# RWKV recurrence of a two-layer trunk: per-pair chunk chain replaced by an affine map per chunk, three head pairs together

## The chip, the cores and the metric

One core of a Trainium2 chip runs the whole program. The metric is device time in microseconds. TensorE (PE) multiplies matrices and loads its stationary operand in separate instructions (PEld); VectorE (DVE) and ScalarE (ACT) do elementwise work; SyncE (SP) issues most DMAs. SBUF and PSUM have 128 partitions; an f32 matmul that is not marked fp32r appears as two MATMUL instructions in the profile, a transpose or an fp32r matmul as one.

## The reference

Two residual layers over 512 tokens of width 1024. The even layer projects the normed input once and splits the columns among MoBA attention (6 heads), RWKV-7 time mixing (6 heads of 64) and memory attention (4 heads); the odd layer has differential attention, HGRN2 and memory attention. The part that is changed is the RWKV recurrence:

```python
def step(st, inp):          # st (head, v, k); all float32
    r_t, w_t, k_t, v_t, a_t, b_t = inp
    sa = jnp.einsum('bhvk,bhk->bhv', st, a_t)
    st = st * w_t[:, :, None, :] + sa[..., None] * b_t[:, :, None, :] + v_t[..., None] * k_t[:, :, None, :]
    return st, jnp.einsum('bhvk,bhk->bhv', st, r_t)
```

with a = -kk, b = kk * a of the layer, a decay w per channel, and after it a group norm per head, a bonus term and a SiLU gate.

## The kernel before

The program is written with a tile framework that orders the instructions of each engine at build time by priority and inserts the waits. The levels, from the first: the RWKV functions run at the top, evictions of projections beside them (`band("e")`), weight loads and their splits next (`band("w")`), norms of attention inputs then (`band("n")`), and projection matmuls (`band("d")`) last, in the order of the string `RWO`. So a projection matmul goes where TensorE has no RWKV instruction to issue.

A projection (`projT`, `projN`, L235) is three fp32r products, hi*hi, hi*lo and lo*hi, each over eight blocks of 128 rows: 24 matmuls of 512 columns for 128 transposed outputs, 96 of 256 columns for a natural chunk. Each chunk of weights is loaded by DMA, split into hi (ACT, L226) and lo (DVE, L227). `RWO` names the chunks: `l0` the low-rank codes and r of pair 0, `k0` k and v of pair 0, `r1` r and k of pair 1, `v1`, `r2`, `v2` likewise; `qm`, `q1` to `q3`, `g0`, `g1` feed attention and gates. The results of r, k, v are evicted by `shift` (L964 on ACT, L968 on DVE). After them, gates `gm` and `ga` are projected in the attention stage, into tiles of a pool that is opened when the RWKV pool is closed.

RWKV handles its six heads as three pairs (two heads of 64 channels on 128 partitions), 512 tokens as 8 chunks of 64. For each pair in turn: `rwkv_prep` builds decays, normed keys, chunk products (L792, L808), masks and transposes; `rwkv_inverse` inverts the 64x64 triangular matrix of each chunk by five doubling levels, two bursts of matmuls each (L856, L863) with VectorE steps between; `rwkv_chain` walks the eight chunks, three 128x128 products a chunk (L888, L894, L900) with evictions between; `rwkv_out` forms the outputs (L914, L916), norms and gates them. The tiles that the next pair needs at once have two buffers, most others one. In the functions below `T`, `V`, `A`, `G` are TensorE, VectorE, ScalarE and GpSimd; `pj("t")` alternates two PSUM tiles, `s2` gives a PSUM tile of two banks.

Of the kernel before, what the change touches and what calls it, by code (L numbers as in the profile page):

```python
# [36 lines left out]
RWO = 'l0 k0 qm r1 v1 q1 r2 g0 v2 q2 q3 g1'  # L37
# [109 lines left out]
def tile_trunk(ctx, tc, x_in, memT_in, w_mem, e_w_in, e_w_out, o_w_in, o_w_out, ln_g, w2_in, a2_in,  # L147
# [588 lines left out]
    def rwkv_prep(rp, q, rkv, lor, rm64, w2a):  # L736
        r, kv = rkv
        k, v = kv[:, :, 0, :], kv[:, :, 1, :]
        t8 = lambda t: t.rearrange("p (c t) -> p c t", t=64)
        bkT = tl(rp, [P, 8, 2, 64], "bkT")  # L740
        a, e2 = bkT[:, :, 0, :], bkT[:, :, 1, :]
        L = tl(rp, [P, S], "lw")
        for m in range(2):
            z = pj("t0")
            T.matmul(z, w2a[:, m, q * P:(q + 1) * P], lor[:, m, :], start=True, stop=True)
            A.activation(a if m else L, t8(z) if m else z, AF.Tanh, scale=0.5, bias=hw0[:, 3 * m + q:3 * m + q + 1])
        A.activation(L, L, AF.Identity, scale=-0.5 * CDEC, bias=ncd)
# [26 lines left out]
        V.tensor_tensor(t8(nr[:, 1]), r, e1[:, :, 1:65], op=OP.mult)
        plc = tl(rp, [P, 8], "plc", bufs=2)
        V.tensor_copy(plc, e1[:, :, 64])
        V.scalar_tensor_tensor(a, a, 1.0, kk, op0=OP.add, op1=OP.mult)
        V.scalar_tensor_tensor(a, a, 0.5, e2, op0=OP.mult, op1=OP.mult)
        V.tensor_tensor(e2, k, e2, op=OP.mult)
        t1 = tl(rp, [P, 8, 64], "t1")  # L780
        V.scalar_tensor_tensor(t1, r, R("rk", q), k, op0=OP.mult, op1=OP.mult)
        bs = pj("t0")
        T.matmul(bs, C("bo"), t1.rearrange("p c t -> p (c t)"), start=True, stop=True)
        bon = tl(rp, [P, S], "bon", bufs=2)
        V.tensor_tensor(t8(bon), t8(bs), v, op=OP.mult)
        hs = [slice(0, 64), slice(64, 128)]
        s = s2()
        for p in range(2):
            for c in range(8):
                o = s[hs[c % 2], p, (c // 2) * 64:(c // 2) * 64 + 64]  # L790
                b_, n_ = bkT[hs[p], c, 0, :], nr[hs[p], 0, c * 64:(c + 1) * 64]
                T.matmul(o, n_ if p else b_, b_ if p else n_, start=True, stop=True)  # L792
        lu = C("lu").rearrange("p (l t) -> p l t", t=64)
        nb = tl(rp, [P, NT, 64], "nb", bufs=2)
        nb2 = tl(rp, [P, NT, 64], "t1")
        sv = s[:, :, 0:256].rearrange("p a (i t) -> p a i t", t=64)
# [3 lines left out]
        nk = tl(rp, [P, 2, 8, 64], "nk")  # L800
        ar = tl(rp, [P, 2, 8, 64], "ar", bufs=2)
        for z in range(2):
            s = s2()
            sv = s.rearrange("p a (c x t) -> p a c x t", x=2, t=64)
            zs = slice(4 * z, 4 * z + 4)
            for c in range(4):
                for p in range(2):
                    T.matmul(sv[:, p, c], bkT[hs[p], 4 * z + c].rearrange("p a t -> p (a t)"),  # L808
                             nr[hs[p], :, (4 * z + c) * 64:(4 * z + c + 1) * 64], start=True, stop=True)
            V.tensor_tensor(nk[hs[1], :, zs], sv[hs[1], :, :, 0, :],  # L810
                            lu[hs[1], 2, None, None, :].to_broadcast([64, 2, 4, 64]), op=OP.mult)
            V.tensor_tensor(ar[:, :, zs], sv[:, :, :, 1, :], C("mr")[:, None, None, :].to_broadcast([P, 2, 4, 64]),
                            op=OP.mult)
        V.tensor_tensor(bkT, bkT, plc[:, :, None, None].to_broadcast([P, 8, 2, 64]), op=OP.mult)
        uv = tl(rp, [P, 2, 8, 64], "uv", bufs=2)
        s = s2()
        sv = s.rearrange("p z (c t) -> p (z c) t", t=P)
        for c in range(8):
            T.transpose(sv[:, c], kv[:, c].rearrange("p a t -> p (a t)"), ident)
        for p in range(2):  # L820
            A.activation(uv[hs[1], p], sv[hs[1], :, hs[p]], AF.Copy)
        bk = tl(rp, [P, 8, P], "bk", bufs=2)
        s = s2()
        sv = s.rearrange("p z (c t) -> p (z c) t", t=P)
        for c in range(8):
            T.transpose(sv[:, c], bkT[:, c].rearrange("p a t -> p (a t)"), ident)
        A.activation(bk.rearrange("p c t -> p (c t)"), s.rearrange("p z t -> p (z t)"), AF.Copy, scale=C("sg"))
        t = pj("t0")
        for p in range(2):
            for c in range(8):  # L830
                m = 4 * p + c // 2
                T.matmul(t[hs[c % 2], m * 64:m * 64 + 64], nk[hs[1], p, c, :], uv[hs[1], p, c, :],
                         start=True, stop=True)
        nv = tl(rp, [P, 8, 64], "nv", bufs=2)
        A.activation(nv.rearrange("p m t -> p (m t)"), t, AF.Copy)
        return dict(bon=bon, nr=nr, pl=plc, nb=nb, nv=nv, ar=ar, uv=uv, bk=bk)

    def rwkv_inverse(rp, st):
        E = st["nb"]
        hs = [slice(0, 64), slice(64, 128)]  # L840
        f = lambda t: t.rearrange("p i t -> p (i t)")
        f3 = lambda t: t.rearrange("p (i t) -> p i t", t=64)
        cm = lambda n, l: C(n).rearrange("p (l t) -> p l t", t=64)[:, l, None, :].to_broadcast([P, NT, 64])
        xx = tl(rp, [P, NT, 64], "xx", bufs=2)
        F = tl(rp, [P, NT, 64], "F", bufs=2)
        V.tensor_tensor(xx, E, cm("lev", 0), op=OP.mult)
        V.tensor_tensor(F, cm("i64", 0), xx, op=OP.subtract)
        for l in range(1, 6):
            R1 = tl(rp, [P, NT, 64], "R1")
            R2 = tl(rp, [P, NT, 64], "R2")  # L850
            V.transpose(f(R1), f(F))
            V.tensor_tensor(R1, R1, cm("tri2", l - 1), op=OP.mult)
            x = pj("t1")
            for i in range(NT):
                for h in hs:
                    T.matmul(x[h, i * 64:i * 64 + 64], E[h, i, :], R1[h, i, :], start=True, stop=True)  # L856
            V.tensor_tensor(R2, F, cm("tri2", l - 1), op=OP.mult)
            xx = tl(rp, [P, NT, 64], "xx", bufs=2)
            V.tensor_tensor(xx, f3(x[:, :256]), cm("lev", l), op=OP.mult)
            x = pj("t1")  # L860
            for i in range(NT):
# [12 lines left out]
        V.tensor_tensor(g64[:, :, 0], F, cm("lu", 0), op=OP.mult)
        A.activation(g64[:, :, 1], f3(x[:, :256]), AF.Copy)
        st["g64"] = g64

    def rwkv_chain(rp, st, Z, Wz):
        hs = [slice(0, 64), slice(64, 128)]
        uv, bk, nr, pl, g64 = st["uv"], st["bk"], st["nr"], st["pl"], st["g64"]  # L880
        nv = st["nv"].rearrange("p (a i) t -> p a i t", a=2)
        cs_ = st["c"] = s2("c")
        for c in range(8):
            i, h = c // 2, c % 2
            W = Wz[h]
            if c:
                w = cs_[:, 0, 0:P]
# [525 lines left out]
```

## Time and profile before

| | us |
|---|---|
| median of 3 runs | 695.09 (694.81 to 695.23) |
| the profiled execution | 695.85 |
| its span, first to last instruction | 694.1 |
| TensorE matmul busy / weight loads | 669.2 (96%) / 557.3 (80%) |
| VectorE / ScalarE busy | 505.5 (73%) / 336.5 (48%) |

A row of a group names line, engine, operation, tiles (out<-in) and shapes (for a matmul stationary rows*columns, output partitions x moving columns), how often, then busy us and mean ns of one, then the idle time before it and what ended it. Matmuls overlap in TensorE's pipeline, so the mean of one is its latency; what it costs in a stream is the distance of starts, which the timeline gives.

### The profile page before, as it was taken

The page shows a single profiled execution, that of the slowest core. Times are in us where ns is not written, and L with a number is a line of the kernel's source. Part 1 is how long each engine was busy: PE and PEld are TensorE (multiplying, and loading weights), DVE is VectorE, ACT ScalarE, POOL GpSimd, SP SyncE. Part 2 cuts the span into 40 slices and gives each one's busy share as a digit, 9 for nine tenths or more (in the row PEclk, how much of TensorE's full clock was granted, in tenths as well). Part 3 has the DMA queues.
Part 4 walks back from the last instruction along what each step waited for, and adds up shares of the span by engine and source line. Part 5 has one row for each costly group of instructions (what it writes and reads, how often), then busy time and mean ns, then how long its engine had stood idle before and what let it go on. Part 6 is the DMA issues. An engine that isn't in the chain of part 4 may idle for free.

```text
span 694.1 us, 14695 instructions
## 1 busy us (share of the span) xinstructions
PE 669.2 (96%) x5748; PEld 557.3 (80%) x5748; DVE 505.5 (73%) x1487; ACT 336.5 (48%) x1009; POOL 7.2 (1%) x24
## 2 busy tenths in 40 slices
PE   8899999999999998999999999899999999999998
PEld 5777877787679876566799988679999977567997
DVE  3996876988795759857765985994737558889853
ACT  5567245262334347534532866544445336568520
POOL 1000000000000000000000000000000000000000
PEclk9999999999999999999999999999999999999999
DMA  8372122111013242010342344003324231000223
GB/s 300 112 192 61 32 61 79 45 35 43 20 36 89 62 126 88 1 38 1 111 161 87 122 128 109 16 3 122 120 64 119 65 92 31 31 1 1 92 61 122
DMA packets 62903, 53.48 MB, mean 77 GB/s; under 512 B 3377, under 2 KB 61041, under 8 KB 62834
## 3 DMA queue, kind: packets, MB, share of 16 engines
q1 hardware_dynamic: 62834, 52.55, 24.8%
q8 instruction: 45, 0.74, 0.5%
q14 instruction: 24, 0.20, 0.1%
HBM read 50.44 MB, written 2.10 MB: 76 GB/s over the span
## 4 chain that ended last, share of the span: by engine, by line
PE 71%; DVE 16%; ACT 7%; issue 2%; DMA 2%; SPq 0%; ACTq 0%; DVEq 0%
PE pj L235 49%; PE s L466 2%; PE c L900 1%; PE t L863 1%; PE t L520 1%; PE t L572 1%; PE t L856 1%; DVE lo L227 1%; ACT pr L547 1%; PE t L1278 1%; PE t L512 1%; PE c L894 1%; PE t L449 1%; DVE act_lo L425 1%; DMA memT<-in_memT_dram 1%
## 5 line engine op out<-in xcount | busy, mean ns | idle before, releaser
L226 ACT ACTIVATE hi<-raw 128x512 fp32r<-128x512 f32 (+2 forms) x164 | 90.7, 597 | 85.4 <-PE pj L235 65.3
L227 DVE TENSOR_TENSOR lo<-raw,hi 128x512 fp32r<-128x512 f32 (+2 forms) x164 | 102.0, 648 | 28.0 <-PE pj L235 24.5
L235 PE MATMUL pj<-hi,act_hi 128*128 128x256 f32 x672 | 105.9, 286 | 0.7 <-ACT act_hi L274 0.5
L235 PE MATMUL pj<-hi,act_lo 128*128 128x256 f32 x672 | 105.3, 285 | 0.0
L235 PE MATMUL pj<-lo,act_hi 128*128 128x256 f32 x672 | 104.7, 285 | 0.0
L235 PEld LDWEIGHTS pj<-hi,act_hi 128*128 128x128 f32 x672 | 90.2, 188 | 3.3 <-ACT act_hi L274 1.2
L235 PEld LDWEIGHTS pj<-hi,act_lo 128*128 128x128 f32 x672 | 90.1, 188 | 1.0 <-issue 0.4
L235 PEld LDWEIGHTS pj<-lo,act_hi 128*128 128x128 f32 x672 | 90.0, 188 | 0.7 <-issue 0.2
L235 PE MATMUL pj<-act_hi,lo 128*128 128x512 f32 (+1 forms) x248 | 73.9, 415 | 0.0
L235 PE MATMUL pj<-act_lo,hi 128*128 128x512 f32 (+1 forms) x248 | 73.8, 415 | 0.0
L235 PE MATMUL pj<-act_hi,hi 128*128 128x512 f32 (+1 forms) x248 | 69.1, 406 | 0.0
L235 PEld LDWEIGHTS pj<-act_lo,hi 128*128 128x128 f32 (+1 forms) x248 | 44.4, 189 | 11.5 <-issue 1.6
L235 PEld LDWEIGHTS pj<-act_hi,hi 128*128 128x128 f32 (+1 forms) x248 | 44.4, 187 | 9.9 <-issue 0.5
L235 PEld LDWEIGHTS pj<-act_hi,lo 128*128 128x128 f32 (+1 forms) x248 | 44.3, 189 | 9.9 <-issue 1.2
L586 DVE TENSOR_TENSOR x<-pj,x 128x256 f32<-128x256 f32 x64 | 27.0, 422 | 34.7 <-PE pj L235 34.5
L617 ACT ACTIVATE sq<-pj 128x64 f32<-128x64 f32 x144 | 30.1, 226 | 26.7 <-DVE nat L492 15.5
L478 ACT ACTIVATE pr<-pr,mx 128x128 f32<-128x128 f32 (+3 forms) x56 | 30.9, 556 | 4.4 <-DVE mx L476 4.0
L617 ACT ACTIVATION_READ_ACCUMULATOR sq<-pj 128x1 f32 x144 | 29.3, 211 | 0.0
L476 DVE CUSTOM_DVE_ANT_0 pr<-s,mask 128x128 f32<-128x128 f32 (+3 forms) x56 | 25.7, 484 | 4.2 <-PE t L512 1.9
L490 ACT ACTIVATE uv<-c 64x64 f32<-64x64 f32 x48 | 10.5, 219 | 34.9 <-PE c L894 34.3
L490 ACT ACTIVATE PT<-t 128x512 f32<-128x512 f32 (+3 forms) x28 | 13.9, 497 | 26.4 <-PE t L563 9.7
L547 ACT ACTIVATE pr<-s,mmx 128x256 f32<-128x256 f32 x32 | 14.8, 484 | 7.6 <-DVE mmx L544 7.6
(388 smaller groups left out, 1087.8 us busy)
## 6 DMA issues: line engine op xcount, KB each, us to landing
raw<-in_o_w_in_dram SPq DMA_DIRECT2D x20, 512.0 KB, 3.7
raw<-in_e_w_in_dram SPq DMA_DIRECT2D x36, 256.0 KB, 3.3
raw<-in_e_w_in_dram SPq DMA_DIRECT2D x10, 512.0 KB, 5.0
x<-in_x_dram SPq DMA_DIRECT2D x8, 512.0 KB, 7.7
raw<-in_o_w_in_dram SPq DMA_DIRECT2D x16, 256.0 KB, 3.6
raw<-in_o_w_out_dram SPq DMA_DIRECT2D x8, 512.0 KB, 3.4
raw<-in_e_w_out_dram SPq DMA_DIRECT2D x4, 512.0 KB, 3.5
raw<-in_w_mem_dram SPq DMA_DIRECT2D x4, 512.0 KB, 3.5
```

The source lines that it names most:

```text
L226: A.activation(hi[:, z, :n], r, AF.Copy)
L227: V.tensor_tensor(lo[:, z, :n], r, hi[:, z, :n].bitcast(F32), op=OP.subtract)
L235: T.matmul(o, lh(k), rh(k), start=c == 0, stop=c == tot - 1)
L425: V.tensor_tensor(act_lo[:, k0:k0 + 4, i * P:(i + 1) * P], tv, hv.bitcast(F32), op=OP.subtract)
L449: T.transpose(t[:, i * P:(i + 1) * P], nat[:, i, c0:c0 + P], ident)
L466: T.matmul(o, qT[a][h, qs], kT[b][h, ks], start=c == 0, stop=c == 2)
L476: V.tensor_tensor_reduce(pr[:, p, :n], s[:, p, :n], mask[0][:, 384 - i * P:512], 1.0, 1e38, op0=OP.add, op1=OP.min, accum_out=mx[:, p:p + 1])
L478: A.activation(pr[:, p, :n], pr[:, p, :n], AF.Exp, bias=mx[:, p:p + 1], scale=-1.0, accum_out=rs[:, p:p + 1])
L490: A.activation(dst, src, AF.Copy)
L547: A.activation(pv[:, p, ii, :], sv[:, p, ii, :], AF.Exp, bias=mx[:, c:c + 1], scale=-1.0, accum_out=rs[:, c:c + 1])
L586: V.tensor_tensor(x[i][:, cs], o, x[i][:, cs], op=OP.add)
L617: A.activation(sq[:, h0 + h], o[:, 64 * (h0 + h):64 * (h0 + h + 1)], AF.Square, accum_out=ss[:, i * nh + h:i * nh + h + 1])
```

## The change

Each chunk's effect on the state is written as an affine map: state' = AT^T state + Z. `rwkv_prep` builds what the maps need for one pair, into tiles `X` that hold all three pairs; the three preparations run first. Then `rwkv_inverse` inverts the chunks of all pairs in one batch (24 blocks in a burst instead of 8), `rwkv_affine` multiplies the inverses out into AT, Z, corrected r and Y, `rwkv_chain` needs one product and one add for each chunk, for three pairs at once, and `rwkv_out` runs for each pair. `RWO` moves `qm`, `q1` and `g0` behind the chunks of r, k and v. The r and k tiles have two buffers, v one. Three memsets on GpSimd go. Added and context lines of the diff, cut to its core (removed lines stand in the functions above):

```diff
+RWO = 'l0 k0 r1 v1 r2 v2 qm q1 g0 q2 q3 g1'
...
+    def rwkv_tiles(rp):
+        return dict(nr=tl(rp, [P, 4, S], "nr3"), pl=tl(rp, [P, 3, 8], "pl3"), bon=tl(rp, [P, 3, S], "bon3"),
+                    nb=tl(rp, [P, 3, NT, 64], "nb3"), NN=tl(rp, [P, 3, 2, NT, P], "NN3"),
+                    BA=tl(rp, [P, 3, 2, NT, P], "BA3"), Z=tl(rp, [P, 3, 7, 64], "Z3"),
+                    Yv=tl(rp, [P, 3, 2, NT, 64], "Yv3"))
+
+    def rwkv_prep(pp, X, q, rkv, lor, rm64, w2a):
...
+        cz = lambda i, h: slice((2 * i + h) * 64, (2 * i + h) * 64 + 64)
+        s = s2("s")
+        sv = s.rearrange("p a (i t) -> p a i t", t=P)
+        for i, h, p in rows:
+            nc_ = cz(i, h)
+            if p:
+                T.matmul(sv[hs[h], p, i, 0:64], n[hs[p], nc_], b[hs[p], nc_], start=True, stop=True)
+                T.matmul(sv[hs[h], p, i, 64:P], b[hs[p], nc_], rs[hs[p], nc_], start=True, stop=True)
+            else:
+                T.matmul(sv[hs[h], p, i], b[hs[p], nc_], nr[hs[p], 0:q + 2:q + 1, nc_], start=True, stop=True)
...
+        V.tensor_tensor(BA[:, :, :, 64:P], sv[:, :, :, 64:P], lub(0), op=OP.mult)
+        s = s2("c")
+        sv = s.rearrange("p a (i t) -> p a i t", t=P)
+        for i, h, p in rows:
+            T.matmul(sv[hs[h], p, i], e2[hs[p], cz(i, h)], nr[hs[p], 0:q + 2:q + 1, cz(i, h)], start=True, stop=True)
+        nk = tl(pp, [P, 2, NT, 64], "t1", bufs=4)
+        V.tensor_tensor(nk, sv[:, :, :, 0:64], lub(2), op=OP.mult)
+        av = tl(pp, [P, 2, NT, 64], "t1", bufs=4)
+        V.tensor_tensor(av, sv[:, :, :, 64:P], lub(0), op=OP.mult)
...
+        for f, dst in ((n, NN[:, :, :, 64:P]), (b, BA[:, :, :, 0:64]), (e2, None)):
+            t = pj("t")
+            for i in range(NT):
+                T.transpose(t[:, i * P:(i + 1) * P], f[:, i * P:(i + 1) * P], ident)
+            if dst is None:
+                A.activation(kt.rearrange("p i t -> p (i t)"), t, AF.Copy)
+            else:
+                A.activation(dst, i2(t), AF.Copy)
+        ph_ = lambda t, p, i: t[:, (p * NT + i) * 64:(p * NT + i) * 64 + 64]
+        for src, dst in ((nk, NN[:, :, :, 0:64]), (av, X["Yv"][:, q])):
+            t = pj("t")
+            for i, h, p in rows:
+                T.matmul(ph_(t, p, i)[hs[h]], src[hs[h], p, i], vt[hs[h], i, hs[p]], start=True, stop=True)
+            A.activation(dst, p2(t), AF.Copy)
+        s = s2("s")
+        for i, h, p in rows:
+            if 2 * i + h < 7:
+                T.matmul(s[hs[p], h, i * 64:i * 64 + 64], kt[hs[h], i, hs[p]], vt[hs[h], i, hs[p]],
                          start=True, stop=True)
...
+        xx, F, R1, R2 = (T4(n) for n in ("xx", "F", "R1", "R2"))
+        V.tensor_tensor(xx, E4, cm("lev", 0), op=OP.mult)
         V.tensor_tensor(F, cm("i64", 0), xx, op=OP.subtract)
         for l in range(1, 6):
...
+            x = x4()
+            for j in range(2 * J):
                 for h in hs:
+                    T.matmul(at(x, h, j), E[h, j], at(R1, h, j), start=True, stop=True)
...
+            for j in range(2 * J):
                 for h in hs:
+                    T.matmul(at(x, h, j), at(xx, h, j), at(R2, h, j), start=True, stop=True)
+            V.tensor_tensor(F, F, x, op=OP.subtract)
...
+                        X["pl"].rearrange("p q c -> p (q c)")[:, :, None].to_broadcast([P, 24, 64]), op=OP.mult)
+        rows = [(i, h, p) for i in range(NT) for p in range(2) for h in range(2)]
+        for q in range(3):
+            NN, BA = X["NN"][:, q], X["BA"][:, q]
+            s = s2("s")
+            for i, h, p in rows:
+                T.matmul(s[hs[h], p, i * P:(i + 1) * P], g[hs[h], q * NT + i, p], NN[hs[h], p, i],
                          start=True, stop=True)
             for p in range(2):
+                o = s[:, p].rearrange("p (i t) -> p i t", t=P)
+                if p:
+                    V.tensor_scalar(NN[:, p], o, -1.0, None, op0=OP.mult)
+                else:
+                    A.activation(NN[:, p], o, AF.Copy, scale=-1.0)
+        for q in range(3):
+            NN, BA = X["NN"][:, q], X["BA"][:, q]
+            s = s2("c")
+            for i, h, p in rows:
+                T.matmul(s[hs[p], h, i * P:(i + 1) * P], NN[hs[h], p, i, 64:P], BA[hs[h], p, i], start=True, stop=True)
+            sv = s.rearrange("p h (i t) -> p h i t", t=P)
+            s = s2("s")
+            for i, h, p in rows:
+                if 2 * i + h < 7:
+                    T.matmul(s[hs[p], h, i * 64:i * 64 + 64], BA[hs[h], p, i, 0:64], NN[hs[h], p, i, 0:64],
+                             start=True, stop=True)
+            d = AT[:, q].rearrange("p (i h) t -> p h i t", h=2)
+            V.tensor_tensor(d, sv[:, :, :, 0:64], d, op=OP.add)
+            for h in range(2):
+                z = X["Z"][:, q, h:7:2]
+                V.tensor_tensor(z, s[:, h, 0:64 * z.shape[1]].rearrange("p (i t) -> p i t", t=64), z, op=OP.add)
+            d = X["nr"][:, q + 1].rearrange("p (i h t) -> p h i t", h=2, t=64)
+            V.tensor_tensor(d, sv[:, :, :, 64:P], d, op=OP.add)
+            t = pj("t").rearrange("p (a i t) -> p a i t", a=2, t=64)
+            for i, h, p in rows:
+                T.matmul(t[hs[h], p, i], BA[hs[h], p, i, 64:P], NN[hs[h], p, i, 0:64], start=True, stop=True)
+            V.tensor_tensor(X["Yv"][:, q], t, X["Yv"][:, q], op=OP.add)
+        return AT
+
+    def rwkv_chain(X, AT):
+        Z = X["Z"]
+        s = s2("s")
+        for c in range(1, 7):
+            o = s[:, c % 2, 0:192].rearrange("p (q t) -> p q t", t=64)
+            for q in range(3):
+                for h in hs:
+                    T.matmul(o[h, q], AT[h, q, c], Z[h, q, c - 1], start=True, stop=True)
+            V.tensor_tensor(Z[:, :, c], o, Z[:, :, c], op=OP.add)
...
+        s = s2("sc"[q % 2])
+        y = s[:, :, 0:256].rearrange("p a (i t) -> p a i t", t=64)
...
+        for c in range(1, 8):
             for p in range(2):
+                T.matmul(y[hs[c % 2], p, c // 2], X["nr"][hs[p], q + 1, c * 64:(c + 1) * 64], X["Z"][hs[p], q, c - 1],
+                         start=True, stop=True)
...
+                                got[n, q] = d = tl(pp, [P, S], n, bufs=1 if n == "v" else 2)
...
             for q in range(3):
+                rwkv_prep(pp, X, q, [got[n, q] for n in "rkv"], lor, rm64, w2a)
+            pps.close()
+            with ExitStack() as ips:
+                ip = pool(ips, "ip")
+                AT = rwkv_affine(ip, X, rwkv_inverse(ip, X))
+                rwkv_chain(X, AT)
+                for q in range(3):
+                    rwkv_out(ip, X, q, sg[3 + q])
```

## Rows read from the trace of the kernel before

**Rows 1.** The page: the engines' busy time, share of the span and instructions.

```profile
PE 669.2 (96%) x5748; PEld 557.3 (80%) x5748; DVE 505.5 (73%) x1487; ACT 336.5 (48%) x1009; POOL 7.2 (1%) x24
```

**Rows 2.** Stretches of the span. Columns: stretch and its length, busy time of each engine (instructions), granted clock, share of DMA, GB/s.

```profile
55.00:262.00 207.00, 202.55 (x1918) 163.78 (x1919) 158.33 (x459) 87.22 (x266) 1.65 (x5) 1.00 0.21 60
262.00:345.00 83.00, 79.52 (x471) 54.35 (x470) 61.75 (x170) 44.10 (x127) 0.00 (x0) 1.00 0.13 38
```

**Rows 3.** Groups of TensorE matmuls from 55 to 262 us, L235 being the projections: one row of three for 512 columns (x96, x96, x94) and one of three for 256 columns (x128 each).

```profile
L235 PE MATMUL pj<-act_hi,lo 128*128 128x512 f32 x96 | 29.5, 417 | 0.0
...
L235 PE MATMUL pj<-lo,act_hi 128*128 128x256 f32 x128 | 21.9, 293 | 0.0
```

**Rows 4.** Timeline of TensorE where projections run alone. Columns: start, duration to the modelled end of the last, engine, line, operation, tiles, stationary and moving shapes, count.

```profile
298.78 2.03 PE L235 MATMUL pj<-act_hi,lo 128*128 128x512 f32 x8
300.65 2.03 PE L235 MATMUL pj<-act_hi,hi 128*128 128x512 f32 x8
...
364.75 0.76 PE L235 MATMUL pj<-hi,act_lo 128*128 128x256 f32 x5
365.35 0.76 PE L235 MATMUL pj<-lo,act_hi 128*128 128x256 f32 x5
```

**Rows 5.** The same timeline at a burst of the inverse (L856 and L863 are its two products), and where one stands beside the 16 instructions of L832: the rows left out are single instructions of both.

```profile
152.48 0.63 PE L235 MATMUL pj<-act_lo,hi 128*128 128x512 f32 x2
153.04 0.68 PE L863 MATMUL t<-R,xx 64*64 64x64 f32 x16
153.65 0.74 PE L235 MATMUL pj<-act_lo,hi 128*128 128x512 f32 x2
...
86.56 0.51 PE L832 MATMUL t<-uv,nk 64*64 64x64 f32 x10
...
87.64 0.62 PE L235 MATMUL pj<-hi,act_lo 128*128 128x256 f32 x3
```

**Rows 6.** The same timeline in the first steps of the first pair's chain.

```profile
106.21 1.17 PE L235 MATMUL pj<-act_hi,lo 128*128 128x512 f32 x4
107.29 0.49 PE L900 MATMUL c<-uv,bk 128*128 128x128 f32 x2
107.53 0.94 PE L235 MATMUL pj<-act_hi,lo 128*128 128x512 f32 x3
108.42 0.49 PE L888 MATMUL c<-Z,nr 128*128 128x128 f32 x2
108.66 0.48 PE L235 MATMUL pj<-act_hi,lo 128*128 128x512 f32 x1
108.97 0.62 PE L235 MATMUL pj<-act_hi,hi 128*128 128x512 f32 x2
109.44 0.41 PE L894 MATMUL c<-W,g 128*128 128x128 f32 x2
109.60 0.72 PE L235 MATMUL pj<-act_hi,hi 128*128 128x512 f32 x2
```

**Rows 7.** The same timeline at the first pair's output, with a burst of the second pair's preparation (L808) behind it, and before these L792 of the first pair (the first of its rows, 32 instructions in all, and the projection after them).

```profile
72.92 0.51 PE L792 MATMUL s<-nr,bkT 64*64 64x64 f32 x10
...
73.83 0.73 PE L235 MATMUL pj<-hi,act_lo 128*128 128x256 f32 x4
...
133.32 1.20 PE L914 MATMUL c<-uv,ar 128*64 128x64 f32 x32
134.45 0.68 PE L916 MATMUL c<-Z,nr 64*64 64x64 f32 x28
135.06 1.16 PE L808 MATMUL s<-nr,bkT 64*128 64x128 f32 x16
136.15 0.68 PE L856 MATMUL t<-R,nb 64*64 64x64 f32 x16
```

**Rows 8.** Groups of VectorE and ScalarE from 55 to 262 us. After the bar: busy us and mean ns of one, idle time before them.

```profile
L904 DVE SCALAR_TENSOR_TENSOR Z<-Z,plc,c 64x64 f32<-64x64 f32 x36 | 10.0, 279 | 7.4 <-PE c L900 6.8
L859 DVE TENSOR_TENSOR xx<-t,cmr 128x256 f32<-128x256 f32 x15 | 6.3, 419 | 4.3 <-PE t L856 4.3
L812 DVE TENSOR_TENSOR ar<-s,cmr 128x512 f32<-128x512 f32 x6 | 4.1, 691 | 0.1
L814 DVE TENSOR_TENSOR bkT<-bkT,plc 128x1024 f32<-128x1024 f32 x3 | 3.6, 1214 | 0.0
...
L490 ACT ACTIVATE uv<-c 64x64 f32<-64x64 f32 x48 | 10.5, 219 | 34.9 <-PE c L894 34.3
```

**Rows 9.** Where the pairs stand: first and last start of the first matmul of a preparation (L745), of its last copy (L835) and of the shifts that evict r, k and v (L964), with min/median/max ns; then single rows of the timeline: first and last instruction of the first pair's inverse, one of the last two of its output, and the last pair's last.

```profile
L745 PE MATMUL t<-lor,w2a x6: 394/485/502, 55.2 to 147.2; 96*128 96x512 f32 x6
L835 ACT ACTIVATE nv<-t x3: 590/592/596, 87.7 to 209.4; 128x512 f32<-128x512 f32 x3
L964 ACT ACTIVATE th<-pj,prm x10: 668/690/692, 48.2 to 202.5; 128x512 f32<-128x512 f32 x9, 64x512 f32<-64x512 f32 x1
...
79.05 0.45 DVE L851 STREAM_TRANSPOSE R<-F 128x256 f32<-128x256 f32 x1
105.38 0.39 ACT L875 ACTIVATE g<-t 128x256 f32<-128x256 f32 x1 [4.58 <-PE t L873]
145.35 0.65 DVE L938 TENSOR_TENSOR Yq<-Yq,bon 128x512 f32<-128x512 f32 x1
260.95 0.68 DVE L939 SCALAR_TENSOR_TENSOR sg<-Yq,sg 128x512 f32<-128x512 f32 x1
```

More of the change, by code (lines that the diff above doesn't have):

```diff
@@ L774, in rwkv_prep @@
[L774 to L778, printed above, removed]
+        V.tensor_tensor(t8(n), t8(kk), e1[:, :, 0:64], op=OP.mult)
+        V.tensor_tensor(t8(rs), t8(r), e1[:, :, 1:65], op=OP.mult)
+        V.tensor_copy(X["pl"][:, q], e1[:, :, 64])
+        V.scalar_tensor_tensor(b, b, 1.0, kk, op0=OP.add, op1=OP.mult)
@@ L779, in rwkv_prep @@
+        V.scalar_tensor_tensor(b, b, 0.5, e2, op0=OP.mult, op1=OP.mult)
         V.tensor_tensor(e2, k, e2, op=OP.mult)
-        t1 = tl(rp, [P, 8, 64], "t1")
+        t1 = tl(pp, [P, S], "t1", bufs=4)
         V.scalar_tensor_tensor(t1, r, R("rk", q), k, op0=OP.mult, op1=OP.mult)
[L782 to L796, printed above, removed]
+        bs = pj("t")
@@ new lines, in rwkv_prep @@
+        T.matmul(bs, C("bo"), t1, start=True, stop=True)
+        V.tensor_tensor(X["bon"][:, q], bs, v, op=OP.mult)
+        vt = tl(pp, [P, NT, P], "lw")
+        t = pj("t")
+        for i in range(NT):
+            T.transpose(t[:, i * P:(i + 1) * P], v[:, i * P:(i + 1) * P], ident)
+        A.activation(vt.rearrange("p i t -> p (i t)"), t, AF.Copy)
+        cz = lambda i, h: slice((2 * i + h) * 64, (2 * i + h) * 64 + 64)
+        s = s2("s")
+        sv = s.rearrange("p a (i t) -> p a i t", t=P)
@@ L799, in rwkv_prep @@
         V.tensor_tensor(nb, nb, nb2, op=OP.add)
[L800 to L832, printed above, removed]
-                         start=True, stop=True)
-        nv = tl(rp, [P, 8, 64], "nv", bufs=2)
@@ L857, in rwkv_inverse @@
             V.tensor_tensor(R2, F, cm("tri2", l - 1), op=OP.mult)
[L858 to L861, printed above, removed]
+            V.tensor_tensor(xx, x, cm("lev", l), op=OP.mult)
+            x = x4()
+            for j in range(2 * J):
                 for h in hs:
-                    T.matmul(x[h, i * 64:i * 64 + 64], xx[h, i, :], R2[h, i, :], start=True, stop=True)
@@ new lines, in rwkv_inverse @@
+            V.tensor_tensor(F, F, x, op=OP.subtract)
+        g = tl(ip, [P, 2, J, 2, 64], "g64")
+        V.tensor_tensor(xx, F, cm("lu", 1), op=OP.mult)
+        x = x4()
+        for j in range(2 * J):
+            for h in hs:
+                T.matmul(at(x, h, j), at(xx, h, j), ident[h, h], start=True, stop=True)
+        V.tensor_tensor(g[:, :, :, 0], F, cm("lu", 0), op=OP.mult)
+        for z in range(2):
+            A.activation(g[:, z, :, 1], x[:, z], AF.Copy)
+        return g.rearrange("p b j a t -> p (b j) a t")
```

185 lines of the change are left out of this document (68 added, 117 removed).

## Prediction

> **What bounds the kernel now.** I read the page first. TensorE is busy 96% of the span [rows 1]. "Busy" is not proof, because the ends of matmuls are modelled, so I looked at start-to-start times in the stretch that the change rewrites: from 55 us, when the first head pair's preparation starts, to 262 us, when the last pair's result is written [rows 2, 9]. In those 207 us the granted clock is 1.00, TensorE's upper level of 2.4 GHz, VectorE is busy 158 us, ScalarE 87 us and DMA 21% [rows 2]; none is full. TensorE issues 286 projection matmuls of 512 columns and 384 of 256 there (the two rows shown and the four like them) [rows 3]. In a stretch with no other work such a matmul follows the last one after 0.234 us (8 in 1.87) and 0.120 us (5 in 0.60) [rows 4]. That makes 286 x 0.234 + 384 x 0.120 = 113 us of projection and leaves 94 us. The RWKV bursts fill nearly all of that, as the bursts costed below show: projections run right up to each burst and right after it. So before 262 us TensorE's queue is the bound, the recurrence's long dependency chain is covered by projections, and an RWKV edit is worth the TensorE time that it takes out or puts in, as long as its own chain ends in time. After 262 us comes the attention stage; TensorE is busy 79.5 of 83 us there [rows 2].
>
> **The price of a burst.** All times are from the last projection start before a burst to the first after it, less 0.234 per projection. An f32 matmul is two instructions. An inverse burst is 16 instructions of 64x64 on two quadrants of the array (rows 0-63 to columns 0-63, and the other halves): 153.65 - 152.48 - 2 x 0.234 = 0.70 us, of which 0.61 from its first start to the next projection [rows 5]. Thirty-two such instructions in a row take 1.08 us, so 16 more cost 0.47: 0.029 each, on top of a fixed 0.15 plus 0.09 at the switch. Where four quadrants take turns, 28 instructions need only 0.61 us (L916), so (0.61 - 0.15) / 28 = 0.017 each [rows 7]. A chain burst, two 128x128 instructions, costs 0.38, 0.43 and 0.24 us in the three shown [rows 6]; over the 52 of the trace that stand alone between projections I count a mean of 0.30, which I take.
>
> **The change, part by part (TensorE, three pairs).**
> *Inverse.* 33 bursts of 16 become 11 of 48, the same instructions: 33 x 0.70 = 23.1 before, 11 x (48 x 0.029 + 0.24) = 17.9 after: **-5.2**.
> *Chain.* 22 bursts a pair, 66 x 0.30 = 19.8, go. Six steps remain for all three pairs, each 12 instructions of 64x64 on two quadrants: 6 x (12 x 0.029 + 0.25) = 3.6: **-16.2**.
> *Output.* L914 and L916 take 135.06 - 133.32 = 1.74 us a pair, L916 alone 0.61 [rows 7]; only its like remains: **-3.4**.
> *Preparation.* Gone a pair: L792 0.91, L808 twice 1.09 [rows 7], L832 1.08 (32 instructions of the inverse's kind), with 0.1 for each switch 4.6. New: the products for `s` (per quadrant pair 32 in a row, 1.08), `e2` on four quadrants (32, 0.69), `nk` and `av` times `vt` (1.08 each), `kt` times `vt` (28 on four, 0.63), with switches 5.1. Transposes stay 16 a pair. **+1.4**.
> *Affine map, new.* A pair: `g` times `NN` 1.08, `NN` times `BA` 0.69, `BA` times `NN` 0.63 and 1.08, switches 0.4: 3.9. **+11.6**.
> Sum: **-11.8 us**.
>
> Of these the unknown is the 64x64 matmul with 128 moving columns (`e2`, half of `s`, `g` times `NN`, `NN` times `BA`), which the trace lacks. Nearest from above is L808, 64 rows by 128 stationary and 128 moving columns: 16 instructions in 1.09 us [rows 7], 0.06 each. At that price a pair costs 1.3 more in `e2`, 1.3 in `NN` times `BA`, 0.9 in `g` times `NN`, 0.3 in `s`: +11.3 in all, and the gain is 0.5. Nearest from below is 0.017 and 0.029. I take the low prices: the projection of 256 moving columns issues every 0.120 us, hardly more than the 0.107 that its columns take at 2.4 GHz, so the load of its 128 stationary columns is hidden, and a load should be here too [rows 4].
> The Trainium skill says otherwise ("TensorE: Matmul & The Clock Gate", Part 3, What overlaps and what doesn't): a weight load overlaps a running matmul only when the row group differs. By that rule load and moving columns add up in each row group and the sum would be near the -0.5; by the rows it is -11.8. The trace speaks against the rule: L235 uses all rows in both, and is not slowed to the sum of the two.
>
> *VectorE and ScalarE.* Inverse: 87 instructions of 0.42 become 29 of 768 elements, by interpolation between 0.42, 0.69 and 1.21 for 256, 512 and 1024 elements some 0.96 [rows 8]: 36.5 to 27.8. Masks: four of 0.69 a pair become three. The chain's 17.4 (10.0 of it L904) becomes 16.7 of affine, chain and output adds. VectorE -11 us; ScalarE loses 48 copies of 0.22 and three wide copies [rows 8] and gains eight a pair, about -7. I cost both at nothing, as TensorE's 113 us of projections cover them; without that cover they would only help.
> *Order.* `qm`, `q1` and `g0` move behind the r, k, v chunks of pairs 1 and 2. The same projections, weight loads on SP's queue (two DMAs each), splits on ScalarE and VectorE, and `qm`'s evictions, squares and norms are issued, only later; `qm` is first needed after 262 us. Nothing, covered by DMA at 21%.
> *New waits.* `v` has one buffer, so v of the next pair is shifted only after the last pair's transposes of v; behind that wait on ScalarE stand weight splits and the preparation's own activations. Two projection accumulators let TensorE go on by one output. ScalarE idles 120 of 207 us, so I take nothing; the price is in the second rival.
>
> **Does the chain end in time?** The first preparation runs from 55.2 to 88.3, 33 us; the third is under way at 147 and ends at 210, as it waits for r, k, v projections, whose last shift is at 202.5 [rows 9], and these now come first. VectorE's part is about 15 us a pair: some fifteen instructions of 512 elements at 0.69, L814's 1.21, the scan and a dozen small ones [rows 8]. Three in turn, 28 to 33 each, end at 139 to 154. One pair's inverse took 79.1 to 105.8 [rows 9], 26.7 us, of which its own instructions on the path are about 16 and waits 10.7; in lockstep 5 x (4 x 0.96 + 2 x 1.54) + 3 + 10.7 = 48. Affine: VectorE 3.5 a pair (its adds at the widths of rows 8) and four bursts in turn, 18. Chain: six steps at 1.2 (22 bursts fill 106 to 133 before [rows 6, 7]), 7. Output: 12.7 for one pair (133.3 to 146.0 [rows 7, 9]), of which VectorE 6.6 with the new add; three 12.7 + 2 x 6.6 = 26. Sum 99 us, so it ends at 238 to 253, beside 250 for TensorE's sum (262 - 12) and 262 before. Filler lasts: about 60 of the 113 us remain at 145.
>
> **Rivals.**
> *Wide products at L808's price:* gain 0.5, 694.6. For it only that row; against it rows 4.
> By the rule of the Trainium skill named above ("TensorE: Matmul & The Clock Gate", Part 3) this is what happens.
> *Lockstep comes too late (slower).* No inverse step starts before the third preparation ends, so single buffers (`bkT`, `lw`, `e1`, `v`) in series set the end. It decides from a preparation of 36 us on (55 + 3 x 36 + 99 = 262). At 40 the end is 274, TensorE runs dry and the time is 695.1 + 12 = 707. For it: 33 us is close, and later pairs took longer; against it: those waited for projections.
> *The recurrence ends later than TensorE's sum but before 262,* at about 256: gain 5, 690.
> *More:* the recurrence ends near 238 and attention starts among projections, so part of the waits there (0.5 to 0.9 us each, the 3.5 idle us of rows 2 and as much hidden) goes too: 18 to 24 less, about 674.
>
> **How the numbers follow.** The profiled execution took 695.85 us, span 694.1; the median is 695.09. 695.85 - 11.8 = 684.05, less 0.76 gives 683.3, so **683 us**. Chances: forecast (677 to 688) 0.53, wide products 0.12, too late 0.13, ends at 256 0.10, more 0.12. The range leaves out most of "too late" and the end of "more": 671 to 695. A measurement tells a change from none at about 0.2%, 1.4 us. Faster: 0.53 + 0.10 + 0.12 and a third of the wide products, 0.79; same 0.08; slower 0.13.
>
> **What would show it.** Right: inverse bursts of 48 in about 1.55 us; six chain bursts of 0.35 to 0.6; `e2` and `NN` times `BA` at 32 in 0.7; the last output near 250, with projections around every burst. Wrong: 32 wide instructions in 1.9 us; TensorE idle before the inverse with the third preparation past 163 us; the RWKV stretch shorter, but attention longer by as much because its projections were used up.

## The result, and the profile after

The changed kernel takes 678.77 us (median of 4, 678.45 to 679.95), the kernel before beside it 695.16: ratio 0.9761, 95% interval 0.9739 to 0.9784. The profiled execution took 678.45 us, 17.4 less than that of before; TensorE is as full as it was [rows 1].

The page's busy line (engine, busy us, share, instructions), then two stretches of the span (end times, length, busy us of PE, PEld, DVE, ACT and POOL, TensorE's clock, DMA share, GB/s): the recurrence to its end, and the attention stage. They answer to [rows 1, 2].

```profile
PE 651.4 (96%) x6192; PEld 551.8 (82%) x6192; DVE 491.7 (73%) x1394; ACT 328.2 (49%) x969; POOL 6.8 (1%) x21
...
55.00:249.00 194.00, 189.40 (x2379) 162.01 (x2379) 144.97 (x365) 77.90 (x223) 2.39 (x5) 1.00 0.23 62
249.00:332.00 83.00, 79.72 (x487) 55.29 (x486) 62.88 (x174) 45.84 (x132) 0.00 (x0) 1.00 0.18 60
```

Busy shares hide where the 17 us went, so here is the timeline at the new bursts: the first matmul of the first preparation, the last burst of the third; an inverse burst; the affine map's three kinds; one output; the last instruction of the recurrence. They answer to [rows 5 to 7, 9].

```profile
54.28 0.70 PE L760 MATMUL t<-lor,w2a 96*128 96x512 f32 x2 [0.80 <-DVE w2a L997]
...
136.58 0.63 PE L847 MATMUL s<-lw,t 64*64 64x64 f32 x26
137.15 1.22 PE L235 MATMUL pj<-lo,act_hi 128*128 128x256 f32 x8
...
143.21 1.61 PE L876 MATMUL c<-R,nb 64*64 64x64 f32 x48
144.75 1.10 PE L235 MATMUL pj<-lo,act_hi 128*128 128x256 f32 x7
...
190.89 1.75 PE L905 MATMUL s<-NN,g 64*64 64x128 f32 x28
192.56 0.98 PE L235 MATMUL pj<-lo,act_hi 128*128 128x256 f32 x6
...
197.76 1.64 PE L905 MATMUL s<-NN,g 64*64 64x128 f32 x26 [0.77 <-DVE NN L910]
...
204.61 1.10 PE L917 MATMUL c<-BA,NN 64*64 64x128 f32 x32 [0.29 <-DVE nr L930]
205.51 0.61 PE L922 MATMUL s<-NN,BA 64*64 64x64 f32 x26
...
217.47 0.68 PE L953 MATMUL s<-Z,nr 64*64 64x64 f32 x28
218.08 0.39 PE L235 MATMUL pj<-hi,act_lo 128*128 128x256 f32 x1
...
248.59 0.69 DVE L975 SCALAR_TENSOR_TENSOR sg<-Yq,sg 128x512 f32<-128x512 f32 x1
```

Read start to start: 48 inverse instructions last 144.75 - 143.21 = 1.54 us; 28 wide ones of `g` times `NN` 192.56 - 190.89 = 1.67; 32 wide ones on four quadrants 0.90. Projections stand around the bursts, and the recurrence ends at 249.3 instead of 261.6.

Where the time went, from the first preparation to the first transposes of the odd layer's HGRN2 (55.2 to 420.8 us before, 54.3 to 403.2 after). For each TensorE instruction I took the time to the next one's start, apart from waits over 0.15 us. A burst is whatever TensorE does between two projections, RWKV's or not. A projection counts 0.113 or 0.222 us, the least steady spacing of its two sizes; what exceeds that is booked to the switch into a burst (last projection before it), to the restart (first projection after it), or to the rest. Worked out from the traces, us:

| | before | after | order alone (e2) | old order (e1) | inverse by pair (e3) | pair by pair (e8) |
|---|---|---|---|---|---|---|
| RWKV instructions | 71.5 | 63.9 | 78.2 | 66.1 | 67.3 | 68.5 |
| switches into bursts | 14.2 | 7.5 | 12.1 | 6.8 | 9.7 | 12.0 |
| restarts after bursts | 12.5 | 7.0 | 10.5 | 6.3 | 8.8 | 10.8 |
| bursts | 142 | 79 | 126 | 70 | 96 | 112 |
| projections | 204.2 | 204.2 | 204.2 | 204.2 | 204.2 | 204.2 |
| their other excess | 9.6 | 11.2 | 10.0 | 11.9 | 10.6 | 11.4 |
| other TensorE work | 46.1 | 47.1 | 46.4 | 48.3 | 46.9 | 46.6 |
| waits | 7.5 | 8.1 | 7.7 | 24.1 | 10.7 | 9.2 |
| total | 365.6 | 348.9 | 369.1 | 367.7 | 358.1 | 362.7 |

Before to after: -7.6 in RWKV instructions, -6.7 in switches, -5.5 in restarts, +3.1 elsewhere. Sixty-three bursts fewer are worth 12.2 us apart from the instructions in them.

### The profile page after: what moved, and what is told of

Read it like the earlier page. It is cut to its first block, busy times and chain, and to the rows that moved or that the text cites. A ratio compares the mean times of both kernels' runs of the same rounds, so it can differ in the third digit from the quotient of the medians.

```text
span 676.2 us, 15423 instructions
## 1 busy us (share of the span) xinstructions
PE 651.4 (96%) x6192; PEld 551.8 (82%) x6192; DVE 491.7 (73%) x1394; ACT 328.2 (49%) x969; POOL 6.8 (1%) x21
## 4 chain that ended last, share of the span: by engine, by line
PE 71%; DVE 17%; ACT 6%; DMA 3%; issue 2%; SPq 0%; ACTq 0%; DVEq 0%
PE pj L235 50%; PE s L466 3%; DMA raw<-in_e_w_in_dram 2%; DVE lo L227 1%; PE t L1306 1%; PE t L520 1%; PE t L572 1%; ACT pr L547 1%; PE s L882 1%; PE c L876 1%; PE t L512 1%; PE t L449 1%; PE t L842 1%; DVE pr L554 1%; ACT hi L226 1%
## 5 line engine op out<-in xcount | busy, mean ns | idle before, releaser
L235 PE MATMUL pj<-hi,act_hi 128*128 128x256 f32 x672 | 104.2, 285 | 0.7 <-ACT act_hi L274 0.5
L235 PE MATMUL pj<-hi,act_lo 128*128 128x256 f32 x672 | 102.8, 284 | 0.0
L235 PE MATMUL pj<-lo,act_hi 128*128 128x256 f32 x672 | 102.2, 284 | 0.0
L235 PEld LDWEIGHTS pj<-hi,act_hi 128*128 128x128 f32 x672 | 89.7, 188 | 3.5 <-ACT act_hi L274 1.2
L235 PEld LDWEIGHTS pj<-hi,act_lo 128*128 128x128 f32 x672 | 89.2, 188 | 1.0 <-issue 0.5
L235 PEld LDWEIGHTS pj<-lo,act_hi 128*128 128x128 f32 x672 | 88.9, 188 | 0.8 <-issue 0.3
L235 PE MATMUL pj<-act_lo,hi 128*128 128x512 f32 (+1 forms) x248 | 71.0, 409 | 0.0
L235 PE MATMUL pj<-act_hi,lo 128*128 128x512 f32 (+1 forms) x248 | 69.5, 409 | 0.0
L235 PE MATMUL pj<-act_hi,hi 128*128 128x512 f32 (+1 forms) x248 | 67.7, 403 | 0.0
L235 PEld LDWEIGHTS pj<-act_hi,lo 128*128 128x128 f32 (+1 forms) x248 | 45.7, 190 | 11.2 <-issue 1.2
L235 PEld LDWEIGHTS pj<-act_hi,hi 128*128 128x128 f32 (+1 forms) x248 | 45.0, 187 | 10.6 <-issue 0.5
L235 PEld LDWEIGHTS pj<-act_lo,hi 128*128 128x128 f32 (+1 forms) x248 | 44.6, 187 | 10.7 <-issue 0.5
L429 ACT ACTIVATE th<-pj 128x512 f32<-128x512 f32 x16 | 9.5, 596 | 30.6 <-PE pj L235 30.6
L547 ACT ACTIVATE pr<-s,mmx 128x256 f32<-128x256 f32 x32 | 14.7, 482 | 7.4 <-DVE mmx L544 7.4
```

What stands on the lines that cost most here:

```text
L235: T.matmul(o, lh(k), rh(k), start=c == 0, stop=c == tot - 1)
L429: A.activation(th, o, AF.Tanh, scale=0.5)
L547: A.activation(pv[:, p, ii, :], sv[:, p, ii, :], AF.Exp, bias=mx[:, c:c + 1], scale=-1.0, accum_out=rs[:, c:c + 1])
```

## The experiments

All against runs of the kernel before on the same chip. The diffs are cut to their core.

| kernel | median us | ratio to before, 95% interval |
|---|---|---|
| after | 678.77 | 0.9739 to 0.9784 |
| e1_old_order | 699.83 | 1.0021 to 1.0079 |
| e2_order_alone | 699.54 | 1.0014 to 1.0069 |
| e8_pair_old_order | 692.14 | 0.9919 to 0.9960 |
| e9_pair_new_order | 696.73 | 0.9974 to 1.0035 |
| e3_pair_inverse | 689.67 | 0.9847 to 0.9946 |
| e4_more_projection | 692.04 | 0.9915 to 0.9979 |
| e5_more_bursts | 700.85 | 1.0044 to 1.0094 |
| e6_no_out_norm | 676.85 | 0.9700 to 0.9786 |
| e7_affine_two_psum | 676.76 | 0.9700 to 0.9762 |
| e10_split_wide | 678.47 | 0.9697 to 0.9774 |
| e11_sum_fp32r | 678.33 | 0.9707 to 0.9762 |
| e12_sum_one_burst | 679.13 | 0.9730 to 0.9778 |

**Does TensorE's work decide, or the recurrence's own chain?** Two kernels add work beside that chain, one shortens it by leaving out the group norm of the output.

```diff
 # e4_more_projection, in the outputs of qm, q1, q2, q3
+for _ in range(8):
+    T.matmul(o, lh(k), rh(k), start=True, stop=True)
 # e5_more_bursts, at every sixth step of the same outputs
+T.matmul(scratch, ident[0:64, 0:64], ident[0:64, 0:64], start=False, stop=False)
 # e6_no_out_norm, in rwkv_out
-mu = tl(sp, [P, 8], "ymu")
...
-V.tensor_tensor(Y, Y, r[:, :, None].to_broadcast([P, 8, 64]), op=OP.mult)
```

> The changed kernel with work added: in each of 16 outputs of qm, q1, q2 and q3 the first projection matmul is issued 8 times more (it starts the accumulation anew each time, so the result stays), 128 matmuls of 256 or 512 columns. They stand in the stream of projections beside the recurrence and are on no chain of it. Theory A: all of it shows, 128 x 0.113 to 0.234, 14 us or more (15 if all are of 256 columns). Theory B (the recurrence's chain decides, TensorE has slack): 0 to 3 us.

Measured +13.3 us (ten runs, 690.4 to 695.9). In the trace 128 x 0.113 = 14.5 us of projection came in and 1.6 us of waits went.

> The changed kernel with work added: in the 16 outputs of qm, q1, q2 and q3 a lone f32 product of 64x64 (two instructions) that nobody reads is put after every sixth projection step, 64 bursts in all. It measures what a burst costs that does nearly no work. My prediction's price of a burst, 0.24 fixed plus 2 x 0.029 = 0.30: 64 x 0.30 = 19 us more. With the restart of the projection after it, which the prediction left out, 0.40: 25.6 us more. If a burst costs only its instructions: 64 x 0.06 = 4 us. Theory B (the recurrence's chain decides): 0 to 3 us.

Measured +22.1 us for 64 bursts of two instructions.

A lone burst between projections in that trace (timeline):

```profile
150.39 0.28 PE L239 MATMUL pj<-hi,act_lo 128*128 128x256 f32 x1
150.59 0.33 PE L237 MATMUL pj<-cident 64*64 64x64 f32 x2
150.85 0.97 PE L239 MATMUL pj<-hi,act_lo 128*128 128x256 f32 x6
```

The projection before it takes 0.20 instead of 0.113 to its successor, the two instructions 0.26. Over all, by the same booking as in the table: +14.7 us between starts of other TensorE instructions, which the lone ones are (0.23 a burst), +5.0 in switches, +5.3 in restarts: 25.0 us, 0.39 a burst, of which 2.6 us of waits and 1.2 of other excess are paid back. My price gave 0.30; the restart, which it left out, is the difference.

> The changed kernel without the group norm of the recurrence's output (mean, variance and scaling left out, three times twelve instructions on VectorE and ScalarE; TensorE keeps its instructions). The recurrence's end comes some 10 to 15 us earlier. Theory A (TensorE's work counts): 0 to 2 us faster. Theory B (the recurrence's end counts): 10 to 15 us faster.

Measured -1.9 us, the upper end of theory A; its interval overlaps that of the changed kernel, so the gain is not clear of noise. The first two outputs end at 226.0 instead of 239.2 and attention's first scores start at 228.9 instead of 249.9 us, yet the last instruction comes only 1.7 us earlier in the trace. That the recurrence would end 10 to 15 us earlier failed, it ends at 245.4, since the last output now waits for the gate that it is multiplied with, whose projection is the last of the list:

```profile
243.99 0.69 DVE L430 SCALAR_TENSOR_TENSOR sg<-th,pj 128x512 f32<-128x512 f32 x1 [3.41 <-ACT th L429]
244.71 0.69 DVE L963 SCALAR_TENSOR_TENSOR sg<-Yq,sg 128x512 f32<-128x512 f32 x1
```

**Which part of the change gains: the order, the affine map, or the lockstep?** Each alone:

```diff
 # e1_old_order: after with the order of before; e2_order_alone: before with this order
-RWO = 'l0 k0 r1 v1 r2 v2 qm q1 g0 q2 q3 g1'
+RWO = 'l0 k0 qm r1 v1 q1 r2 g0 v2 q2 q3 g1'
 # e8_pair_old_order, e9_pair_new_order: after, pair by pair (tiles for two pairs, not three)
 for q in range(3):
     rwkv_prep(pp, X, q, [got[n, q] for n in "rkv"], lor, rm64, w2a)
-AT = rwkv_affine(ip, X, rwkv_inverse(ip, X))
-rwkv_chain(X, AT)
-for q in range(3):
+    g = tl(ip, [P, NT, 2, 64], "g64")
+    rwkv_inverse(ip, X, q, g)
+    rwkv_chain(X, q, rwkv_affine(ip, X, q, g))
     rwkv_out(ip, X, q, sg[3 + q])
 # e3_pair_inverse: after, with only the inverse by pair
+for q in range(3):
+    rwkv_inverse(ip, X, q, g)
```

> The changed kernel with the chunks in the order of the kernel before (qm and q1 ahead of the r, k, v chunks they stood ahead of, v2 late); the RWKV code stays new. Theory A (TensorE's work counts, and the recurrence's chain only if it ends after its projections are used up): TensorE's work is the same, so as long as projections last the time is within 1 us of the changed kernel. The third preparation now waits for about 34 us more of projections and ends near 172 instead of 138 us; the 111 us from there to the end of the recurrence (138 to 249 in the changed kernel) then end near 283, projections are used up before, and TensorE idles: 695 to 710, 15 to 30 us above the changed kernel. Theory B (only the chain's end counts): the same direction, the full 34 us, 713. If the order does not matter at all: 678 to 680.

Measured 699.8, 21 us above the changed kernel: theory A. The third preparation ends at 169.4 and the recurrence at 276 (forecast 172 and 283). Windows of the trace (columns as above):

```profile
255.00:262.00 7.00, 0.29 (x3) 0.05 (x1) 6.37 (x19) 1.82 (x3) 0.00 (x0) 0.84 0.40 116
262.00:275.00 13.00, 4.59 (x17) 2.99 (x17) 8.64 (x23) 2.93 (x5) 0.00 (x0) 0.50 0.16 50
275.00:277.00 2.00, 2.00 (x5) 1.36 (x5) 2.00 (x4) 1.04 (x2) 0.00 (x0) 0.53 0.30 121
277.00:290.00 13.00, 11.61 (x91) 8.96 (x91) 10.30 (x23) 7.50 (x25) 0.00 (x0) 1.00 0.23 81
```

and its timeline there:

```profile
254.66 0.63 PE L971 MATMUL t<-cident,Y 128*128 128x128 f32 x4
...
263.10 1.11 PE L971 MATMUL t<-cident,Y 128*128 128x128 f32 x4 [7.81 <-DVE Y L968]
265.08 1.12 PE L449 MATMUL t<-cident,qn 128*128 128x128 f32 x4 [0.87 <-ACT Yq L973]
271.56 1.12 PE L971 MATMUL t<-cident,Y 128*128 128x128 f32 x4 [5.36 <-DVE Y L968]
273.55 1.12 PE L449 MATMUL t<-cident,qn 128*128 128x128 f32 x4 [0.87 <-ACT Yq L973]
274.87 2.33 PE L235 MATMUL pj<-act_hi,hi 128*128 128x512 f32 x5 [0.21 <-DVE sg L430]
```

The projections are used up at 255 us with two of the three outputs still to be normed; VectorE works alone and TensorE's waits grow by 16.0 us. When TensorE starts again after 7.8 idle us, the granted clock reads 0.50, the lower level of 1.2 GHz, and the same four transposes last 1.11 instead of 0.63 us.

> The kernel before with the new order of the chunks alone, RWKV code as before. Theory A: TensorE's work is that of before, so 695 within 1.5 us, unless r, k, v of the next pair wait for buffers that the pair before still holds, which blocks TensorE behind two projection accumulators: then some us slower. If the order by itself brought the gain (rival): 678 to 685.

Measured +4.4 us: no gain. Bursts of several pairs now meet (126 instead of 142), which saves 4.2 us of switches and restarts, but the RWKV instructions take 6.7 us more from start to start. Why they do was not tested.

> The affine map without the lockstep: each pair's inverse, affine map, chain and output right behind its own preparation, with the chunks in the order of the kernel before. Against the changed kernel TensorE has 22 inverse bursts more (7.0 us by the trace of the kernel with the inverse by pair) and 12 chain bursts more (12 x 0.42, the price of a lone burst measured in the kernel with 64 of them: 5.0). Theory A (TensorE's work counts, each pair's chain is covered by projections as in the kernel before): 678.8 + 12 = 691, 688 to 694. If the affine map by itself brought the gain: 679 to 683. If it brought nothing: 695.

Measured 692.1, in theory A's range. The affine map alone takes 3.0 us off the RWKV instructions and 30 bursts away (switches and restarts -4.0), and gives back 1.7 us in waits and 2.4 elsewhere.

> The same, pair by pair, with the new order of the chunks. Theory A: TensorE's work is that of the kernel with the old order, so within 3 us of it (in the kernel before the order alone gave +3 to +4). If the new order is what pays: 679 to 683.

Measured 696.7, +4.6 where at most 3 were expected: as with the old code (+4.4), the order costs by itself. In the traces, 3.5 us apart, 2.3 are waits of TensorE; what causes them is open.

> The changed kernel with the inverse taken for one pair at a time: 33 bursts of 16 products instead of 11 of 48, the same 528 products. Theory A: 22 bursts more, each with a fixed 0.24 us and a restart of the next projection of 0.1 us, so TensorE has 7 to 8 us more: 685 to 687 as long as the chain ends beside projections. With my prediction's price of a burst (0.24 without the restart) 5 us: 684. Theory B (the chain's length decides): the three inverses in turn take 3 x 20 to 3 x 27 us instead of 47, 13 to 34 us later: 692 or more.

Measured +10.9 (9.2 in the traces). TensorE's part is as forecast: the inverse's instructions +3.1, switches +2.2, restarts +1.7, 7.0 us in all. The rest is theory B's in a small dose: the inverses end 21 us later, and the recurrence, which ends at 266.5, adds 2.6 us of waits. Medians put together, us:

| code | old order | new order |
|---|---|---|
| before | 695.2 | 699.5 |
| affine map, pair by pair | 692.1 | 696.7 |
| affine map, in lockstep | 699.8 | 678.8 |

The order is worth 21 us in the lockstep and costs 4 to 5 without; the lockstep is worth 18 us with the new order and costs 8 with the old.

**The price of the wide products.**

```diff
 # e10_split_wide, in rwkv_affine
-T.matmul(s[hs[h], p, i * P:(i + 1) * P], g[hs[h], q * NT + i, p], NN[hs[h], p, i],
-         start=True, stop=True)
+for z in (slice(0, 64), slice(64, P)):
+    T.matmul(s[hs[h], p, i * P + z.start:i * P + z.stop], g[hs[h], q * NT + i, p],
+             NN[hs[h], p, i, z], start=True, stop=True)
 # e7_affine_two_psum, in rwkv_affine
-s = s2("s")
+s = s2("sc"[q % 2])
```

> The changed kernel with each product of g and NN (64 x 64 stationary, 128 moving columns) issued as two products of 64 moving columns, 64 instructions instead of 32 a pair. If the time goes by moving columns (theory A): 64 x 0.029 + 0.15 = 2.0 us a pair instead of 1.75, time within 1 us of the changed kernel. If a wide product had a hidden load and cheap columns, as I predicted: 64 instructions would cost 0.9 us a pair more, 2.8 in all.

Measured 678.5, no difference. Its timeline:

```profile
192.18 1.90 PE L906 MATMUL s<-NN,g 64*64 64x64 f32 x56
194.00 0.97 PE L235 MATMUL pj<-lo,act_hi 128*128 128x256 f32 x6
```

56 narrow instructions take 194.00 - 192.18 = 1.82 us where 28 wide ones of the same columns take 1.67; less the fixed 0.15, 0.030 and 0.054 each. Twice the moving columns cost 1.8 times, so the time goes by moving columns; there is little of a load beside them.

> The changed kernel with the three products of g and NN in turn in two PSUM tiles instead of one. In the changed kernel TensorE waits there for the copy out of the one tile, 0.77 us at one of them. Theory A: the two waits go, 1 to 2 us faster. If the waits only move to the next product (the second tile is needed there anyway): within 0.5 us.

Measured 2.0 us below the changed kernel. The intervals of the two ratios overlap; the traces agree: over the stretch of the table -1.8 us, of which affine instructions -1.2 and waits -0.5. It has the lowest median of all that were run. The three products now run on:

```profile
191.18 1.75 PE L905 MATMUL s<-NN,g 64*64 64x128 f32 x28
192.76 1.91 PE L905 MATMUL c<-NN,g 64*64 64x128 f32 x32
194.50 1.80 PE L905 MATMUL s<-NN,g 64*64 64x128 f32 x30
```

**The format of the operands.** On top of that kernel, the sum over a head in the projections' format:

```diff
 # e11_sum_fp32r; e12_sum_one_burst: the same with the remainder t1r[1] first
-T.matmul(bs, C("bo"), t1, start=True, stop=True)
+t1r = [tl(pp, [P, S], "t1", F32R, bufs=4) for _ in range(2)]
+A.activation(t1r[0], t1, AF.Copy)
+V.tensor_tensor(t1r[1], t1, t1r[0].bitcast(F32), op=OP.subtract)
+for c in range(2):
+    T.matmul(bs, X["bo"], t1r[c], start=c == 0, stop=c == 1)
```

> The kernel with two PSUM tiles in the affine map, and the product that sums r times k over each head (128 x 128 stationary, 512 moving columns, f32, two instructions, 0.95 us a pair in the changed kernel) in the projections' format: its moving operand is split into a rounded part and a remainder, two instructions of the form of the projections, with one copy on ScalarE and one subtraction on VectorE more a pair. If the moving columns of f32 pass at half the rate of the projections' format (theory A): 2 x 0.234 instead of 0.95, 0.5 us a pair, 1.4 in all: 675.3. If the rate does not depend on the format: 676.8, or later by the longer preparation.

> The kernel before this one with the two products of the sum in the other order: the remainder, which is ready last, goes first, so that both stand in one burst (there they were two bursts 1.3 to 1.5 us apart). If a burst has a price of its own (theory A): one burst less a pair, 0.81 down to 0.23 + 0.33 = 0.56 us a pair in the products, 0.2 for each switch and restart, 1.4 in all: 676 to 677, about the time of the kernel with two PSUM tiles alone or 1 us below. If bursts have no price: no difference, 678.

Measured 678.3 and 679.1: neither gained, though each instruction became faster. The sum in the changed kernel, then in the one-burst form with its neighbours:

```profile
70.80 1.02 PE L796 MATMUL t<-t,cmr 128*128 128x512 f32 x2
71.75 0.33 PE L812 MATMUL s<-nr,bkT 64*64 64x128 f32 x2
```

```profile
73.37 0.28 PE L814 MATMUL s<-nr,bkT 64*64 64x64 f32 x2
73.91 0.73 PE L800 MATMUL t<-t,bor 128*128 128x512 f32 x2 [0.26 <-DVE t L798]
74.57 0.27 PE L813 MATMUL s<-bkT,nr 64*64 64x64 f32 x1
```

The pair of instructions falls from 0.95 to 0.66 us. But TensorE's queue has them in the midst of the products for `s`, and waits there for VectorE's remainder: between starts those products take 5.0 us for three pairs instead of 3.0. In the other form the two instructions became two bursts 1.3 to 1.5 us apart. So it is shown that the sum's own instructions are faster in that format, and the gain is not.

## Why the prediction was right, and where its steps were off

The forecast case came: TensorE's work in the stretch set the time, the recurrence's end was covered. 683 stood for 678.8; the terms up to the recurrence's end, counted as the prediction counted them (instructions and switch, no restart; TensorE's waits in and before a burst are in it), us:

| term | predicted | measured |
|---|---|---|
| inverse | -5.2 | -5.5 |
| chain | -16.2 | -17.9 |
| output | -3.4 | -3.7 |
| preparation | +1.4 | -1.2 |
| affine map | +11.6 | +15.4 |
| sum | -11.8 | -12.8 |
| restarts after bursts | not counted | -5.3 |
| all else | 0 | +0.7 |
| total | -11.8 | -17.4 |

**The bound** held: work beside the chain showed nearly whole (e4, e5), a shorter output did not (e6). Had "More" been the cause, e6 should have gained; the attention stage did get some 5 us shorter, but because 4.7 us of its projections had been done earlier.

**The missing term is the restart.** "From the last projection start before a burst to the first after it" stops one instruction early: that first projection starts its successor some 0.1 us late. Up to the recurrence's end 103 such spacings sum to 9.8 us of excess before and 46 to 4.4 after. The rows held it: in [rows 6] the lone projection at 108.66 needs 0.31 us to its successor at 108.97, where [rows 4] give 0.234. The three chain bursts read there, 0.38, 0.43 and 0.24, were taken over whole rows, and each holds the restart after the burst before it: from the last projection start, the third is 0.17.

**The affine map was mis-sized at the wide products.** I took 0.029 on the diagonal quadrants; it is 0.054 (1.67 us for 28). On four quadrants I took 0.017; 32 take 0.90 us, 0.023. That is 32 x 0.025 = 0.80 and 0.90 - 0.69 = 0.21 a pair, 3.0 us in all; another 1.1 us of the term are the two waits that the fence above shows (0.77 and 0.29), and fewer switches than costed give some back. The rival named L808's 0.06, and on two quadrants that was nearly right, as was its sign, 32 wide instructions in 1.9 us (32 x 0.054 + 0.15); on four it was not, so the affine map lost 3.0 us and not the 6.6 (1.3 + 0.9 a pair) of the rival. The failed argument is that on projections of 256 moving columns: they are in another format than these f32 products. A wide f32 product stood in the trace of before, the sum over a head, 512 columns (timeline):

```profile
126.55 1.12 PE L783 MATMUL t<-t,cmr 128*128 128x512 f32 x2
127.51 0.38 PE L888 MATMUL c<-Z,nr 128*128 128x128 f32 x2
```

Its two instructions take 127.51 - 126.55 = 0.96 us, where two projections of 512 need 2 x 0.234 = 0.47. The Trainium skill's rule weighed there ("TensorE: Matmul & The Clock Gate", Part 3, What overlaps and what doesn't) would add a load to the moving columns; e10 shows almost none.

**Preparation** saved 1.2 instead of costing 1.4, 2.0 without the waits. Its new products take 4.5 us a pair between starts, as costed, but those removed were dearer than the single rows I read: over the trace of before L792 takes 1.30 us a pair (0.91 costed) and L808 2.56 (2.18).

**The chain's end.** Third preparation 137.9 (139 to 154 predicted), inverse to 191.1, affine map to 208.4, chain to 215.8, outputs to 249.3. The parts from the preparation on took 53 (48), 17 (18), 7 (7) and 33 (26), which is 12 us more than forecast; the preparations ended 1 to 16 us earlier than forecast, so the end still lay in the range, 238 to 253. That two errors offset each other there is luck. The outputs took longer because VectorE, busy 30.0 of the 34 us from 216 to 250, also norms and rotates q and k there.

**Order at nothing** was right only for the sum. The rival "lockstep comes too late" had the right mechanism; its place was the order, not the preparation: with the old order (e1) it gave 699.8, and there the clock's fall came on top.

## What to carry to other kernels

Price a small burst between long matmuls from the last long one before it to the second one after it; where TensorE is full, each burst less paid 0.2 us here beside its instructions. Take a price from a row of the same format as well as the same shape. Lockstep and the order that feeds it are one change: neither gains alone, and the lockstep pays only while other work lasts beside its long serial start.

## What the runs showed of the hardware

Moving columns of f32 pass at about half the rate of the projections' format at equal shape: in the changed kernel the first instruction of the sum starts its successor after 0.428 us, a projection of 512 columns after 0.234. The sum in the projections' format steps by 0.33 (e12), switch and restart included, where the f32 pair takes 0.43 and 0.52. A wide f32 instruction takes 0.054 us where two quadrants take turns and 0.023 where four do, so quadrants do work side by side at this width too. In e1 the granted clock read 0.50 while TensorE issued bursts of four transposes at 263.10, 265.08, 271.56 and 273.55 us and five projections from 274.87 on, and 1.00 again from 276.9 us on.
